# A transformer block on one core: the SSD branch's product kept in four PSUM banks over two passes of its channels

## Chip, cores, metric

One core of one Trainium2 chip. The metric is the device time of one execution in microseconds; three runs of the kernel before gave a median of 601.98 us (601.45 to 602.56).

## What is computed

One block on 256 tokens with 1024 channels, all in float32. Cut to what matters here:

```python
y_ssd  = gated_group_rmsnorm(y_ssd, z, ssd_norm)          # 2048 channels, 4 groups of 512
merged = sigmoid(gate_a) * (y_attn @ w_attn_branch) + sigmoid(gate_b) * (y_ssd @ w_ssd_branch)
x = x + merged @ w_out
x = x + hier_moe(rmsnorm(x, ffn_norm), ...)               # router, top-2 of 32 SwiGLU experts, 96 MiB of weights
```

The product `y_ssd @ w_ssd_branch` sums over 2048 channels and gives 1024 columns. The group norm of the fourth group of channels is the last thing known of its left operand.

## The kernel before

**Products in three passes.** A weight arrives raw (SP issues its transfer, L163), in pieces of 128 rows of the contracted dimension; ACT casts each piece to its high part (L174), and the remainder, the low part, is a subtraction (L178), by DVE for even pieces and by POOL for odd ones. The piece with its two parts is the tile `w_hl`. A product takes three matmuls per piece: high by high, high by low, low by high. `wide_chunk` (L302) makes 512 columns for both tiles of 128 tokens, in two PSUM banks: 8 pieces x 2 token tiles x 3 passes = 48 matmuls. It runs them in an order in which the second token tile follows the first by some pieces.

**The SSD branch's product S** (L842 to L865). Four wide chunks, in the order (i=0, c=0), (i=0, c=1), (i=1, c=0), (i=1, c=1): i is the half of the 2048 channels, c the half of the 1024 columns. Here they are called S1 to S4. `tab[t, c]` holds, for token tile t, the attention branch's part `ta` and the gate's tanh `tb`. For every chunk and token tile DVE computes `mg = (tb + 1) * ps` from PSUM (L848). For i=0 POOL adds that to `ta` in SBUF (L850). For i=1 DVE adds `ta` (L852), PE transposes the sum in four steps into a PSUM bank `ps_mT` (L855), and ACT and DVE split that into `mT` (L860, L861), the left operand of the next product.

**The last group's norm** (`ssd_tail`, L781 to L800) runs while S1 and S2 do, since only S3 and S4 need it: PE sums squares (`ps_n`, L785), DVE scales (`nv`, L787), POOL takes the power -1/2 (L101), PE spreads the result over the partitions (`ps_r`, L791), DVE multiplies (`yg`, L797) and splits (`yT`, L800).

**The product with w_out** (L886 to L928), names `ps_o`: 512 columns as a wide chunk (c=0), then 256 (c=2) and 256 (c=3, one token tile after the other). DVE adds each to x (`x_sb`, L889, L909), ACT squares the sum for the norm (`sqo`, L913), PE transposes it (`ps_hf`, L917), ACT and DVE scale it (`xT`, L923, L921), PE forms the router's logits (`ps_lg`, L927).

**Routing and experts** (from L951). Per token tile a chain of small DVE operations: the sum of squares (`ms`, L954), an inverse root by three Newton steps (names `fr0`, `fr1`, L112 to L123), `logit` (L956), maxima, `sel`, ranks on PE (`ps_rk`), slots (`Dm`, L976). Then for eight groups of four experts PE gathers tokens (L1046), multiplies by the gate and up weights (`pgu`, L1053) and the down weights (`py`, L1113). The experts' weights (`we`, L292) come through SP's queue into buffers that earlier tiles give back: the transfer into a buffer waits until its last reader is done.

**PSUM** has 8 banks: three behind the tag "mm" (pool `pmm`, in rotation) and five by name (pool `pacc`: acc00, acc01, acc10, acc11, pgu). `ps_mT` uses acc10 for t=0 and pgu for t=1, `ps_lg` acc00, `ps_hf` acc01 (and acc11 for c=3, t=1).

**Order of the work.** The program names tiles and operations; a scheduler sets the order on each engine from its own estimate of times, and within one engine the instructions run in that order. An edit at one place can therefore change the order on all engines after it.

Of the kernel before, what the change touches and what calls it, by code (L numbers as in the profile page):

```python
# [11 lines left out]
F32 = mybir.dt.float32  # L12
# [8 lines left out]
P = 128  # L21
T = 256
D = 1024
KD = 8
# [25 lines left out]
def block_kernel(ctx, tc, xin, idn, ngain, catt, cprep, cssd, cmoe, cwr, wsm, wwide, win, wgu, wdn, out, dbg=None):  # L50
    nc = tc.nc
    pe, act, dve, pool = nc.tensor, nc.scalar, nc.vector, nc.gpsimd
# [3 lines left out]
    pmm = ctx.enter_context(tc.tile_pool(name="pmm", bufs=3, space=PSUM))  # L56
# [87 lines left out]
    for t, k in TORD:  # L144
        i = pe.transpose(ps_h[k // 2][:, k % 2, t * P:(t + 1) * P], x_sb[:, t, k * P:(k + 1) * P], ident)
# [66 lines left out]
    for step in PRO:  # L212
        if step[0] == "g":
            g_part(int(step[1]))
        else:
            w, k = (w0 if step[0] == "0" else w1), int(step[1])
# [85 lines left out]
        mm3(tm_regions(w, src, [ps[:, t, :] for t in range(2)]))  # L302
        return ps

    def wide_chunk(name, src, lag, mid=None):


        w = pairs(next_w(), slice(0, 512))
        ps = [pmm.tile([P, 512], F32, tag="mm", name="ps_" + name) for t in range(2)]
        lhs = [pairs(src, slice(t * P, (t + 1) * P)) for t in range(2)]  # L310
        steps = sorted([(k + lag * t + 0.5 * t, t, k) for t in range(2) for k in range(KD)])
        for n, (_, t, k) in enumerate(steps):
            if n == KD and mid:
                mid()
            for i, (a, b) in enumerate(PASSES):
                pe.matmul(ps[t], lhsT=lhs[t][k][:, a], rhs=w[k][:, b], start=k == 0 and i == 0,  # L316
                          stop=k == KD - 1 and i == 2)
        return ps

    def cm_chunk(name, src=hT_all):  # L320
# [518 lines left out]
    xp = ctx.enter_context(tc.tile_pool(name="xp", bufs=NX, reuse_waits="tile"))  # L839
    pacc = ctx.enter_context(tc.tile_pool(name="pacc", bufs=1, space=PSUM, reuse_waits="tile"))  # L840

    for i in range(2):  # L842
        for c in range(2):
            ps = wide_chunk("S", yT[2 * i:2 * i + 2], LAG)
            for t in range(2):
                ta, tb = tab[t, c][:, 0], tab[t, c][:, 1]
                m = mo2.tile([P, 512], F32, tag="y", name="mg")
                dve.scalar_tensor_tensor(m, tb, 1.0, ps[t], op0=ALU.add, op1=ALU.mult)  # L848
                if i == 0:
                    pool.tensor_add(ta, m, ta)  # L850
                    continue
                dve.tensor_add(m, m, ta)  # L852
                pt = pacc.tile([P, 2, 2, P], F32, tag=("acc10", "pgu")[t], name="ps_mT")
                for k in range(4):
                    pe.transpose(pt[:, k // 2, k % 2, :], m[:, k * P:(k + 1) * P], ident)  # L855
                if t == 0:
                    mT += [bigt([P, 2, 2, T], F32R, f"mT{2 * c + j}", "G") for j in range(2)]
                for j in range(2):
                    hl = mT[2 * c + j][:, :, :, t * P:(t + 1) * P]
                    act.copy(hl[:, 0], pt[:, j])  # L860
                    dve.tensor_sub(hl[:, 1], pt[:, j], hl[:, 0].bitcast(F32))  # L861
            if i:
                prefetch(PF1[2 * c] + PF1[2 * c + 1])
# [9 lines left out]
    pool.memset(on16, 1.0)  # L873
    ssq = mo.tile([P, 2, 4], F32, name="ssq")
    pre = mo.tile([P, 2], F32, name="pre")
    ps_lg = pacc.tile([P, 2, 36], F32, tag="acc00", name="ps_lg")

    def warm2(n, after):

# [5 lines left out]
    for c in range(4):  # L885
# [4 lines left out]
        elif c == 2:  # L890
            ps = tm_chunk(next_w(), mT, "o")
# [9 lines left out]
        for ts in ((0,), (1,)) if c == 3 else ((0, 1),):  # L901
            tt = slice(ts[0], ts[-1] + 1)
            nt = len(ts)
            if c == 3:
                mm3(regions[ts[0]:ts[0] + 1])
            phf = pacc.tile([P, 2, nt, P], F32, tag=f"acc{ts[0]}1", name="ps_hf")
            xT = mo2.tile([P, 2, nt, P], F32, tag="y", name="xT")
            if c > 1:
                dve.scalar_tensor_tensor(x1[:, tt, o], ps[ts[0]].unsqueeze(1) if c == 3 else ps, 0.5, x_sb[:, tt, o],  # L909
                                         op0=ALU.mult, op1=ALU.add)  # L910
            for t in ts:
                sq = mo2.tile([P, 256], F32, tag="dc", bufs=1, name="sqo")
                act.activation(sq, x1[:, t, o], AF.Square, accum_out=ssq[:, t, c:c + 1])  # L913
            for kk in range(2):
                for t in ts:
                    k = 2 * c + kk
                    pe.transpose(phf[:, kk, t - ts[0], :], x1[:, t, k * P:(k + 1) * P], ident)  # L917
            for kk in range(2):
                k = 2 * c + kk
                if kk:  # L920
                    dve.tensor_scalar(xT[:, kk], phf[:, kk], fgain[:, k:k + 1], None, op0=ALU.mult)  # L921
                else:
                    act.activation(xT[:, kk], phf[:, kk], AF.Copy, scale=fgain[:, k:k + 1])  # L923
            for kk in range(2):
                for t in ts:
                    k = 2 * c + kk
                    last_lg = pe.matmul(ps_lg[:, t, :], lhsT=xT[:, kk, t - ts[0], :], rhs=wr[:, k, :],  # L927
                                        start=k == 0 and t == 0, stop=k == KD - 1 and t == 1)  # L928
# [93 lines left out]
        pe.transpose(ps_mr, mr, ident)  # L1022
        dve.tensor_reduce(mi, ps_mr, axis=AX.X, op=ALU.max)


    def pt_(shape, name):
        return pmm.tile(shape, F32, tag="mm", name=name)

    ring = list(etags)
    for q in range(8):  # L1030
# [292 lines left out]
```

## Time and profile before

| what | value |
|---|---|
| median of 3 runs | 601.98 us |
| profiled execution, its own time | 601.8 us |
| span of its trace | 600.0 us |
| mean granted clock | 0.982 |
| busy: PE, DVE, ACT, POOL | 562.6, 328.2, 273.5, 252.6 us |
| moved by DMA | 159.27 MB, mean 265 GB/s |

PE's matmuls cover 94% of the span, but the span has stages with different limits: projections, SSD and attention until about 320 us, S from 318 to 365 us, the product with w_out to 393 us, routing to 400 us, experts to the end. Each stage is read for itself, by the timeline of an engine and by the windows. A row of the trace with x4 for fp32 matmuls by the router, for `ps_n` and for `ps_r` stands for two instructions of the program.

### The profile page before, as it was taken

The page shows a single profiled execution, that of the slowest core. Times are in us where ns is not written, and L with a number is a line of the kernel's source. Part 1 is how long each engine was busy: PE and PEld are TensorE (multiplying, and loading weights), DVE is VectorE, ACT ScalarE, POOL GpSimd, SP SyncE. Part 2 cuts the span into 40 slices and gives each one's busy share as a digit, 9 for nine tenths or more (in the row PEclk, how much of TensorE's full clock was granted, in tenths as well). Part 3 has the DMA queues.
Part 4 walks back from the last instruction along what each step waited for, and adds up shares of the span by engine and source line. Part 5 has one row for each costly group of instructions (what it writes and reads, how often), then busy time and mean ns, then how long its engine had stood idle before and what let it go on. Part 6 is the DMA issues. An engine that isn't in the chain of part 4 may idle for free.

```text
span 600.0 us, 9955 instructions
## 1 busy us (share of the span) xinstructions
PE 562.6 (94%) x3605; PEld 403.0 (67%) x3605; DVE 328.2 (55%) x705; ACT 273.5 (46%) x633; POOL 252.6 (42%) x256
## 2 busy tenths in 40 slices
PE   8999999999999998999999999999988898896986
PEld 5878768799898996899877777963543452340412
DVE  4459975799994768789786676462112111210101
ACT  7467557658885768768774445410000000000001
POOL 4897695675854345565677764300000000000000
PEclk9999999999999997999999999999989999997999
DMA  6745245363344467343737669999999999999994
GB/s 264 245 156 170 94 143 176 108 205 127 125 137 145 135 217 330 106 157 130 276 126 298 213 225 415 389 336 416 421 414 412 419 417 414 413 419 419 411 415 175
DMA packets 35811, 159.27 MB, mean 265 GB/s; under 512 B 4144, under 2 KB 5808, under 8 KB 27184
## 3 DMA queue, kind: packets, MB, share of 16 engines
q1 hardware_dynamic: 34464, 157.30, 69.6%
q10 hardware_dynamic: 1296, 1.30, 0.7%
q8 instruction: 30, 0.49, 0.3%
q14 instruction: 21, 0.17, 0.1%
HBM read 157.54 MB, written 1.05 MB: 264 GB/s over the span
## 4 chain that ended last, share of the span: by engine, by line
PE 51%; DMA 28%; DVE 7%; POOL 6%; issue 4%; ACT 3%; ACTq 0%; SPq 0%; POOLq 0%; DVEq 0%
DMA we<-wgu 19%; PE ps_xs L263 8%; PE ps_z L263 8%; PE ps_g L316 5%; DMA we<-wdn 4%; PE ps_A L316 4%; POOL w_hl L178 3%; DMA w_raw<-wwide 3%; PE pgu L1053 2%; PE ps_q L316 2%; PE ps_S L316 2%; PE ps_o L263 2%; PE py L1113 2%; DVE w_hl L178 2%; PE po L565 2%
## 5 line engine op out<-in xcount | busy, mean ns | idle before, releaser
L178 POOL TENSOR_TENSOR w_hl<-w_raw,w_hl 128x512 fp32r<-128x512 f32 (+1 forms) x107 | 153.6, 1441 | 75.4 <-ACT w_hl L174 57.0
L174 ACT CAST w_hl<-w_raw 128x512 fp32r<-128x512 f32 (+1 forms) x212 | 125.8, 618 | 63.3 <-DMA w_raw<-wwide 16.3
L178 DVE TENSOR_TENSOR w_hl<-w_raw,w_hl 128x512 fp32r<-128x512 f32 (+1 forms) x105 | 97.5, 931 | 44.4 <-ACT w_hl L174 43.8
L1053 PE MATMUL pgu<-we,xg 128*32 128x512 f32 x512 | 65.6, 616 | 4.9 <-DMA we<-wgu 4.8
L1071 POOL TENSOR_TENSOR dc<-Dm,cmr 128x128 f32<-128x128 f32 x16 | 6.1, 401 | 147.8 <-DVE Dm L976 132.2
L263 PE MATMUL ps_xs<-hT,w_hl 128*128 128x256 f32 x384 | 52.6, 290 | 0.0
L316 PE MATMUL ps_g<-w_hl,gT 128*128 128x512 f32 x192 | 49.5, 400 | 1.6 <-POOL w_hl L178 1.4
L263 PE MATMUL ps_z<-hT,w_hl 128*128 128x256 f32 x384 | 50.8, 285 | 0.0
L263 PEld LDWEIGHTS ps_xs<-hT,w_hl 128*128 128x128 f32 x384 | 49.0, 196 | 2.6 <-issue 2.6
L263 PEld LDWEIGHTS ps_z<-hT,w_hl 128*128 128x128 f32 x384 | 47.5, 191 | 0.7 <-issue 0.7
L316 PE MATMUL ps_S<-w_hl,yT 128*128 128x512 f32 x192 | 45.5, 393 | 1.4 <-DVE w_hl L178 1.4
L1053 PEld LDWEIGHTS pgu<-we,xg 128*32 128x32 f32 x512 | 15.3, 111 | 43.6 <-issue 26.1
L316 PEld LDWEIGHTS ps_g<-w_hl,gT 128*128 128x128 f32 x192 | 34.9, 188 | 11.2 <-POOL w_hl L178 1.9
L316 PEld LDWEIGHTS ps_S<-w_hl,yT 128*128 128x128 f32 x192 | 35.7, 188 | 9.6 <-DVE w_hl L178 1.9
L1049 DVE TENSOR_TENSOR xg<-ps_g,cmoe 128x512 f32<-128x512 f32 (+2 forms) x18 | 11.4, 631 | 56.1 <-PE ps_g L1046 56.0
L1046 PEld LDWEIGHTS ps_g<-Dm,x_sb 128*128 128x128 f32 x256 | 31.0, 191 | 15.0 <-issue 11.3
L1091 DVE SCALAR_TENSOR_TENSOR ac<-th,pgu 128x256 f32<-128x256 f32 x8 | 3.4, 421 | 63.3 <-ACT th L1089 63.3
L1113 PE MATMUL py<-we,aTt 128*32 128x512 f32 (+1 forms) x272 | 34.0, 626 | 3.8 <-DVE aTt L1099 2.1
L1046 PE MATMUL ps_g<-Dm,x_sb 128*128 128x128 f32 x256 | 33.4, 280 | 0.0
L1124 ACT COPY y<-py 128x512 f32<-128x512 f32 (+1 forms) x9 | 4.9, 539 | 61.7 <-PE py L1113 61.7
L1089 ACT ACTIVATE th<-pgu,rs 128x256 f32<-128x256 f32 x8 | 3.8, 474 | 63.1 <-PE pgu L1053 63.1
L1128 PE MATMUL acc<-y,dcT 128*128 128x512 f32 (+1 forms) x68 | 30.7, 577 | 1.7 <-DVE y L1126 1.6
(308 smaller groups left out, 978.8 us busy)
## 6 DMA issues: line engine op xcount, KB each, us to landing
we<-wgu SPq DMA_DIRECT2D x42, 1024.0 KB, 13.9
w_raw<-wwide SPq DMA_DIRECT2D x60, 512.0 KB, 3.9
we<-wdn SPq DMA_DIRECT2D x25, 1024.0 KB, 13.8
w_raw<-win SPq DMA_DIRECT2D x44, 512.0 KB, 3.6
we<-wgu SPq DMA_DIRECT2D x44, 512.0 KB, 10.6
we<-wdn SPq DMA_DIRECT2D x14, 512.0 KB, 10.2
x_sb<-xin SPq DMA_DIRECT2D x2, 512.0 KB, 4.4
w_raw<-wsm SPq DMA_DIRECT2D x1, 512.0 KB, 5.7
```

Source lines behind the costliest of these rows:

```text
L174: return act.copy(self.hl[i][:, 0], self.raw[i])
L178: return eng.tensor_sub(hl[:, 1], self.raw[i], hl[:, 0].bitcast(F32))
L263: pe.matmul(ps, lhsT=lhs[k][:, a], rhs=rhs[k][:, b], start=j == 0 and k == 0 and i == 0, stop=j == len(regions) - 1 and k == KD - 1 and i ...
L316: pe.matmul(ps[t], lhsT=lhs[t][k][:, a], rhs=w[k][:, b], start=k == 0 and i == 0, stop=k == KD - 1 and i == 2)
L565: pe.matmul(po[64 * jj:64 * jj + 64], lhsT=v_sb[:, kt, j * HD:(j + 1) * HD], rhs=PTs[jj][kt], start=kt == 0, stop=kt == t)
L1046: pe.matmul(ps[:, kk, :], lhsT=x1[:, t, (k + kk) * P:(k + kk + 1) * P], rhs=Dm[:, t].rearrange("p e j -> p (e j)"), start=t == 0, stop=t == 1)
L1049: dve.tensor_tensor(xg[:, ks, :], ps, fgain[:, ks].unsqueeze(2).to_broadcast([P, n, P]), op=ALU.mult)
L1053: i = pe.matmul(pgu[32 * e:32 * e + 32, :], lhsT=xg[:, k, 32 * e:32 * e + 32], rhs=wg[k][e], start=k == 0, stop=k == KD - 1, tile_position ...
L1071: pool.tensor_tensor(dc[:, t], Dm[:, t], cmr[:, t, 4 * q:4 * q + 4].unsqueeze(2).to_broadcast([P, 4, NSLOT]), op=ALU.mult)
L1113: i_py = pe.matmul(py[32 * e:32 * e + 32, :], lhsT=aTt[:, f, 32 * e:32 * e + 32], rhs=wd[2 * n + f][e][:, c], start=f == 0, stop=f == 1, t ...
L1124: act.copy(y, py)
L1128: pe.matmul(acc[t][n][:, c], lhsT=dcT[:, t * P:(t + 1) * P], rhs=y, start=False, stop=q == 7 and c.stop == 512)
```

## The change

The sums over i are kept in PSUM: four accumulators, `sacc[0]` in two "mm" banks for c=0 and `sacc[1]` in acc10 and pgu for c=1. A chunk of i=0 starts the sum and doesn't close it, that of i=1 goes on and closes it. The operations of L848 and L850 for i=0 go; for i=1 they stay as they were (`mg`, then the addition of `ta` by DVE). `ps_mT` moves to acc11 (t=0) and acc10 (t=1, the bank of c=1, t=0). `ps_lg` and the first `ps_hf` are only allocated earlier. Lines behind L302 shift by 4 or more.

```diff
@@ wide_chunk @@
+    def wide_chunk(name, src, lag, mid=None, into=None, part=None):
         w = pairs(next_w(), slice(0, 512))
-        ps = [pmm.tile([P, 512], F32, tag="mm", name="ps_" + name) for t in range(2)]
+        ps = into or [pmm.tile([P, 512], F32, tag="mm", name="ps_" + name) for t in range(2)]
...
-                pe.matmul(ps[t], lhsT=lhs[t][k][:, a], rhs=w[k][:, b], start=k == 0 and i == 0,
-                          stop=k == KD - 1 and i == 2)
+                pe.matmul(ps[t], lhsT=lhs[t][k][:, a], rhs=w[k][:, b], start=k == 0 and i == 0 and part != 1,
+                          stop=k == KD - 1 and i == 2 and part != 0)
@@ S @@
+    sacc = [[pt_([P, 512], f"ps_S0{t}") for t in range(2)]]
+    ps_lg = pacc.tile([P, 2, 36], F32, tag="acc00", name="ps_lg")
+    ps_hf0 = pacc.tile([P, 2, 2, P], F32, tag="acc01", name="ps_hf")
+    sacc.append([pacc.tile([P, 512], F32, tag=n, name=f"ps_S1{t}") for t, n in enumerate(("acc10", "pgu"))])
     for i in range(2):
         for c in range(2):
-            ps = wide_chunk("S", yT[2 * i:2 * i + 2], LAG)
+            ps = wide_chunk("S", yT[2 * i:2 * i + 2], LAG, into=sacc[c], part=i)
+            if i == 0:
+                continue
             for t in range(2):
                 ta, tb = tab[t, c][:, 0], tab[t, c][:, 1]
                 m = mo2.tile([P, 512], F32, tag="y", name="mg")
                 dve.scalar_tensor_tensor(m, tb, 1.0, ps[t], op0=ALU.add, op1=ALU.mult)
-                if i == 0:
-                    pool.tensor_add(ta, m, ta)
-                    continue
                 dve.tensor_add(m, m, ta)
-                pt = pacc.tile([P, 2, 2, P], F32, tag=("acc10", "pgu")[t], name="ps_mT")
+                pt = pacc.tile([P, 2, 2, P], F32, tag=("acc11", "acc10")[t], name="ps_mT")
...
-            phf = pacc.tile([P, 2, nt, P], F32, tag=f"acc{ts[0]}1", name="ps_hf")
+            phf = ps_hf0 if c == 0 else pacc.tile([P, 2, nt, P], F32, tag=f"acc{ts[0]}1", name="ps_hf")
```

The scheduler moves instructions as well, from the end of S1 on. Up to there all engines' orders are the same. Three places are shown.

**PE at the end of S1**: S1 and S2 with the norm's two small products. Before (the names yT_2054 and yT_2055 are the first half of the channels, yT_2056 and yT_2057 the second):

```order
L316 MATMUL ps_S<-w_hl,yT_2055 128x512 x14
L316 MATMUL ps_S<-w_hl,yT_2054 128x512 x4
L316 MATMUL ps_S<-w_hl,yT_2055 128x512 x4
L785 MATMUL ps_n<-ones,ysum 128x1 x2
L316 MATMUL ps_S<-w_hl,yT_2054 128x512 x8
L316 MATMUL ps_S<-w_hl,yT_2055 128x512 x4
L316 MATMUL ps_S<-w_hl,yT_2054 128x512 x11
L791 MATMUL ps_r<-ident,nv 128x128 x2
L316 MATMUL ps_S<-w_hl,yT_2054 128x512
L316 MATMUL ps_S<-w_hl,yT_2055 128x512 x16
L316 MATMUL ps_S<-w_hl,yT_2056 128x512
```

Now (ps_S_3973 and ps_S_3974 are the accumulators of c=0, ps_S_3977 and ps_S_3978 those of c=1):

```order
L320 MATMUL ps_S_3973<-w_hl,yT_2055 128x512 x2
L320 MATMUL ps_S_3974<-w_hl,yT_2055 128x512 x2
L789 MATMUL ps_n<-ones,ysum 128x1 x2
L795 MATMUL ps_r<-ident,nv 128x128 x2
L320 MATMUL ps_S_3977<-w_hl,yT_2054 128x512 x12
L320 MATMUL ps_S_3978<-w_hl,yT_2054 128x512 x3
```

Before, 23 matmuls of S2 stood between `ps_n` and `ps_r`; now `ps_r` is right behind `ps_n`, and all of S2 is behind both.

**PE at the end of the product with w_out.** Before:

```order
L263 MATMUL ps_o_4573<-w_hl,mT_4351 128x256 x3
L927 MATMUL ps_lg<-cwr,xT 128x36 x2
L263 MATMUL ps_o_4573<-w_hl,mT_4351 128x256
L927 MATMUL ps_lg<-cwr,xT 128x36 x2
L917 MATMUL ps_hf<-ident,x_sb 128x128 x4
L263 MATMUL ps_o_4573<-w_hl,mT_4351 128x256 x2
L263 MATMUL ps_o_4573<-w_hl,mT_4352 128x256 x6
L927 MATMUL ps_lg<-cwr,xT 128x36 x4
L917 MATMUL ps_hf<-ident,x_sb 128x128 x4
L927 MATMUL ps_lg<-cwr,xT 128x36 x4
```

Now (ps_o_4557 is the last token tile's sum for c=3):

```order
L263 MATMUL ps_o_4557<-w_hl,mT_4228 128x256 x4
L263 MATMUL ps_o_4557<-w_hl,mT_4337 128x256 x6
L263 MATMUL ps_o_4557<-w_hl,mT_4338 128x256 x6
L934 MATMUL ps_lg<-cwr,xT 128x36 x4
L924 MATMUL ps_hf<-ident,x_sb 128x128 x6
L934 MATMUL ps_lg<-cwr,xT 128x36 x4
L924 MATMUL ps_hf<-ident,x_sb 128x128 x2
L934 MATMUL ps_lg<-cwr,xT 128x36 x4
```

Before, the logits of c=0 to 1 and the transposes `ps_hf` of c=2 stood ahead of the last matmuls of `ps_o`; now four `ps_lg` and four `ps_hf` more are behind them.

**DVE at the same place.** Before:

```order
L119 SCALAR_TENSOR_TENSOR fr0a<-fr0y,fr0h 128x1
L921 TENSOR_SCALAR xT<-ps_hf,cmoe 128x256
L123 SCALAR_TENSOR_TENSOR fr0y<-fr0a,fr0y 128x1
L909 SCALAR_TENSOR_TENSOR x_sb<-ps_o_4573,x_sb 128x256
L119 SCALAR_TENSOR_TENSOR fr0a<-fr0y,fr0h 128x1
L123 SCALAR_TENSOR_TENSOR fr0y<-fr0a,fr0y 128x1
L971 COPY r<-fr0y 128x1
L954 TENSOR_SCALAR ms_4731<-ssq,pre 128x1
L112 TENSOR_SCALAR fr1i<-ms_4731 128x1
L116 TENSOR_SCALAR fr1h<-ms_4731 128x1
L921 TENSOR_SCALAR xT<-ps_hf,cmoe 128x128
```

Now:

```order
L113 TENSOR_SCALAR fr0y<-fr0i 128x1
L119 SCALAR_TENSOR_TENSOR fr0a<-fr0y,fr0h 128x1
L123 SCALAR_TENSOR_TENSOR fr0y<-fr0a,fr0y 128x1
L961 TENSOR_SCALAR ms_4715<-ssq,pre 128x1
L119 SCALAR_TENSOR_TENSOR fr0a<-fr0y,fr0h 128x1
L112 TENSOR_SCALAR fr1i<-ms_4715 128x1
L116 TENSOR_SCALAR fr1h<-ms_4715 128x1
L123 SCALAR_TENSOR_TENSOR fr0y<-fr0a,fr0y 128x1
L113 TENSOR_SCALAR fr1y<-fr1i 128x1
L119 SCALAR_TENSOR_TENSOR fr0a<-fr0y,fr0h 128x1
L119 SCALAR_TENSOR_TENSOR fr1a<-fr1y,fr1h 128x1
L928 TENSOR_SCALAR xT<-ps_hf,cmoe 128x256
```

Before, `xT` of c=2 (128x256) stood ahead of the last addition to x and of `ms` of the second token tile (ms_4731). Now it stands behind both (the addition is the row ahead of these, ms_4715 the second tile's sum) and behind seven steps of the two inverse roots.

## Rows read from the trace of the kernel before

**Rows 1.** The page, part 2: granted clock in tenths, GB/s; 40 slices
```profile
PEclk9999999999999997999999999999989999997999
GB/s 264 245 156 170 94 143 176 108 205 127 125 137 145 135 217 330 106 157 130 276 126 298 213 225 415 389 336 416 421 414 412 419 417 414 413 419 419 411 415 175
```

**Rows 2.** The page, part 4: the chain of waits that ended last, by line
```profile
DMA we<-wgu 19%; PE ps_xs L263 8%; PE ps_z L263 8%; PE ps_g L316 5%; DMA we<-wdn 4%; PE ps_A L316 4%; POOL w_hl L178 3%; DMA w_raw<-wwide 3%; PE pgu L1053 2%; PE ps_q L316 2%; PE ps_S L316 2%; PE ps_o L263 2%; PE py L1113 2%; DVE w_hl L178 2%; PE po L565 2%
```

**Rows 3.** Windows: length, each engine's busy time, clock, DMA share, GB/s
```profile
400.00:404.00 4.00, 4.00 (x35) 3.01 (x33) 2.02 (x13) 0.34 (x3) 0.76 (x2) 1.00 0.73 235
```

**Rows 4.** Timeline of SP: start, length (us), operation, count
```profile
390.47 12.54 SPq L292 DMA_DIRECT2D we<-wdn  x6
```

**Rows 5.** Timeline of PE, 329 to 369 us; in brackets idle time before
```profile
330.09 0.50 PE L785 MATMUL ps_n<-ones,ysum 128*128 128x1 f32 x4
345.59 14.85 PE L316 MATMUL ps_S<-w_hl,yT 128*128 128x512 f32 x64 [1.43 <-DVE w_hl L178]
360.27 1.03 PE L855 MATMUL ps_mT<-ident,mg 128*128 128x128 f32 x8
361.06 4.60 PE L316 MATMUL ps_S<-w_hl,yT 128*128 128x512 f32 x19
365.50 2.43 PE L316 MATMUL ps_o<-w_hl,mT 128*128 128x512 f32 x10
...
368.16 3.48 PE L316 MATMUL ps_o<-w_hl,mT 128*128 128x512 f32 x14 [0.23 <-POOL w_hl L178]
```

**Rows 6.** Timeline of POOL, 327 to 332 us
```profile
327.18 3.43 POOL L178 TENSOR_TENSOR w_hl<-w_raw,w_hl 128x512 fp32r<-128x512 f32 x2
...
330.87 0.71 POOL L101 TENSOR_TENSOR nv<-nv,mhalf 128x2 f32<-128x2 f32 x1
```

**Rows 7.** DVE at 336 us (timeline); the page's group of its lo parts
```profile
336.53 0.53 DVE L871 TENSOR_TENSOR trs<-cwr,ident 128x128 bf16<-128x128 f32 x1 [4.55 <-DMA cwr<-cwr]
...
L178 DVE TENSOR_TENSOR w_hl<-w_raw,w_hl 128x512 fp32r<-128x512 f32 (+1 forms) x105 | 97.5, 931 | 44.4 <-ACT w_hl L174 43.8
```

**Rows 8.** The two lines that the change drops for two chunks, all instances
```profile
L848 DVE SCALAR_TENSOR_TENSOR mg<-tab,ps_S x8: 672/675/681, 330.7 to 368.6; 128x512 f32<-128x512 f32 x8
...
L850 POOL TENSOR_TENSOR tab<-mg,tab x4: 1293/1294/1296, 332.8 to 347.5; 128x512 f32<-128x512 f32 x4
```

**Rows 9.** Timeline of PE, 390 to 402 us
```profile
390.82 0.53 PE L927 MATMUL ps_lg<-cwr,xT 128*128 128x36 f32 x4
391.18 0.63 PE L917 MATMUL ps_hf<-ident,x_sb 128*128 128x128 f32 x4
391.57 1.20 PE L263 MATMUL ps_o<-w_hl,mT 128*128 128x256 f32 x8
392.61 0.98 PE L927 MATMUL ps_lg<-cwr,xT 128*128 128x36 f32 x8
...
401.56 1.06 PE L1053 MATMUL pgu<-we,xg 128*32 128x512 f32 x8
```

**Rows 10.** Timeline of DVE, 391 to 396 us
```profile
391.17 0.15 DVE L112 TENSOR_SCALAR fr0i<-ms 128x1 int32<-128x1 int32 x1
...
391.99 0.22 DVE L119 SCALAR_TENSOR_TENSOR fr0a<-fr0y,fr0h 128x1 f32<-128x1 f32 x1
...
392.83 0.41 DVE L909 SCALAR_TENSOR_TENSOR x_sb<-ps_o,x_sb 128x256 f32<-128x256 f32 x1
...
393.89 0.21 DVE L954 TENSOR_SCALAR ms<-ssq,pre 128x1 f32<-128x1 f32 x1
...
394.60 0.34 DVE L921 TENSOR_SCALAR xT<-ps_hf,cmoe 128x128 f32<-128x128 f32 x1
...
395.58 0.25 DVE L956 SCALAR_TENSOR_TENSOR logit<-ps_lg,fr0y,cmoe 128x36 f32<-128x36 f32 x1
```

**Rows 11.** A gap on PE (timeline) and the granted clock after it (windows)
```profile
229.55 0.65 PE L765 MATMUL py<-e,xdt 128*64 128x256 f32 x4 [1.78 <-DVE e L750]
...
232.00:236.00 4.00, 4.00 (x22) 3.51 (x19) 4.00 (x11) 4.00 (x10) 0.73 (x1) 0.50 1.00 413
```

More of the change, by code (lines that the diff above doesn't have):

```diff
@@ L303, in tm_chunk, with pt_ @@
         return ps
-    def wide_chunk(name, src, lag, mid=None):
+    def pt_(shape, name):
+        return pmm.tile(shape, F32, tag="mm", name=name)
+    def wide_chunk(name, src, lag, mid=None, into=None, part=None):
         w = pairs(next_w(), slice(0, 512))
-        ps = [pmm.tile([P, 512], F32, tag="mm", name="ps_" + name) for t in range(2)]
+        ps = into or [pmm.tile([P, 512], F32, tag="mm", name="ps_" + name) for t in range(2)]
         lhs = [pairs(src, slice(t * P, (t + 1) * P)) for t in range(2)]
@@ L875, in block_kernel @@
     pre = mo.tile([P, 2], F32, name="pre")
-    ps_lg = pacc.tile([P, 2, 36], F32, tag="acc00", name="ps_lg")
     def warm2(n, after):
@@ L1023, in combine @@
         dve.tensor_reduce(mi, ps_mr, axis=AX.X, op=ALU.max)
-    def pt_(shape, name):
-        return pmm.tile(shape, F32, tag="mm", name=name)
     ring = list(etags)
```

## The prediction

> **What bounds the kernel now.** I read the 40 slices first [rows 1]. From the 28th slice on, all but the last move 411 to 421 GB/s: the experts' weights fill the DMA engines. The chain of waits says the same: its largest piece is the transfer `we<-wgu`, 19% of the span [rows 2]. So the last third is bound by bytes, and PE's busy share there is no bound.
>
> A stage bound by bytes would hide anything done ahead of it, if it never ran dry. It does. Between 400 and 404 us the DMA share is 0.73, at 235 GB/s [rows 3]. SP's queue shows why: the issues of `we<-wdn` that begin at 390.47 us take 12.54 us for six, because the last waits for a buffer until 402.7 us, when the first `pgu` matmuls, begun at 401.56 us, give back weights [rows 4, 9]. What had been issued before has landed by then. From there to the end, the remaining bytes follow the release by the first `pgu`. **So the time moves one for one with the start of `pgu`**, that is, with the chain S, product with w_out, routing, gather. Earlier prefetches gain nothing: they only make the queue run dry sooner. A gain larger than the dry spell would stop paying; none as large is in sight.
>
> In that chain PE is the engine to follow. From S1 to the last `ps_o` it runs almost without a gap: one of 1.43 us before 345.59 us, for a low part from DVE, and one of 0.23 us before 368.16 us, for one from POOL [rows 5]. DVE was late at the first because it had stood 4.55 us at `trs`, whose constants land at 336.5 us, with the parts of the weights behind it [rows 7].
>
> **The change, part by part.**
>
> *Removed work.* Four `mg` of 0.675 us on DVE, 2.7 us, and four additions of 1.293 us on POOL, 5.2 us [rows 8]. PE waited for none of the additions; the results of i=0 were wanted only at i=1, and the matmuls are the same 192. I cost this at nothing by itself: the matmuls cover it. It frees DVE and POOL for the low parts of S2 to S4, which matters only where PE waits for them: 1.43 and 0.23 us, 1.66 us at most.
>
> *PE at the end of S1.* In the row of before, four matmuls of S2 stand ahead of `ps_n` at 330.09 us. At (360.27 - 345.59)/64 = 0.229 us each [rows 5], S1 ends at 330.09 - 0.92 = 329.17 us. Now `ps_n` starts there and ends 0.50 us later, at 329.67 us. Then `nv` has to pass POOL, which is busy with low parts until 327.18 + 3.43 = 330.61 us and does the same there as before; its power takes 0.71 us [rows 6]. So it ends between 331.3 (started at once) and 331.6 us (started at 330.87 as before). The order puts `ps_r` directly behind `ps_n`, so PE has nothing to run until then: **a gap of 1.65 to 1.95 us**, where before 23 matmuls covered it. I take 1.9, since a small memset stands ahead of the power. With `ps_r` in 0.4 us, S2 starts at 332.0 us.
>
> From there 144 matmuls at 0.229 us are 33.0 us; four transposes, at (361.06 - 360.27)/8 = 0.1 us, add 0.4. S ends at 365.4 us against 365.50 us [rows 5], but four transposes more follow in the next stage (0.4 us): +0.3 us. This holds only without the stall of 1.43 us. The low part that it waited for is now behind `nv`, `yg`, half of `yT` and `trs`, with six low parts next to it; after 337.1 us, where `trs` ends [rows 7], two or three operations at the group's mean of 0.93 us [rows 7] bring the first low part by 340 us. PE wants it with its 38th matmul of S2, at 332.0 + 38 x 0.229 = 340.7 us. So no stall, by 0.7 us; with two inputs delayed it could be 1 us of stall: a bound for the range.
>
> *The banks held.* The transposes of c=0, t=1 now go to the bank of S4's first token tile, and so wait for the `mg` that empties it. The trace's price for that is one `mg`, 0.675 us [rows 8]; nine matmuls of the other token tile and seven of `ps_o` stand in between, 16 x 0.229 = 3.7 us. I put it at nothing. The Trainium skill, page "PSUM — Partial Sum Buffer", section "Summary: rules for kernel authors", says to empty PSUM promptly because it is small, which speaks against holding four banks over two chunks. By that rule the sum would be larger by up to 0.7 us; by the rows the wait lies under other matmuls, and I keep nothing.
>
> *Queues.* SP's issues stay in their order but for two experts' transfers that change places, and come up to 1.8 us earlier (the 1.43 us stall and the freed POOL); by the first part this is worth nothing.
>
> *The product with w_out.* Its 0.23 us for POOL [rows 5] should go with POOL's additions: -0.2 us (bounds -0.23 and 0).
>
> *The tail.* Before, the last `ps_o` ended at 392.61 us, where `ps_lg` follows, and `logit` started at 395.58: 2.97 us [rows 9, 10]. Now four `ps_lg` (twice 391.18 - 390.82 = 0.36 us) and four `ps_hf` (391.57 - 391.18 = 0.39 us) [rows 9] come behind the last `ps_o`, which is 1.1 us earlier. But behind it DVE goes on in this order: the addition to x; `ms` of that tile, 393.89 - 392.83 = 1.06 us later; seven steps of the roots at (391.99 - 391.17)/5 = 0.16 us, 1.1 us [rows 10]; then `xT` of c=2, some 0.5 us. That is 2.8 us after the last `ps_o`, with 0.1 us to start. Then eight more steps, 1.2 us, and two `xT` of c=3, 0.7 us: 4.7 us. From the last `xT` to `logit` the rows have 395.58 - 394.60 = 0.98 us, of which the `xT` itself is 0.34: 5.3 us. So +2.3 us, -1.1 us: +1.2 us. The two tiles' routing steps now run in pairs, and of the 6.0 us from `logit` to `pgu` [rows 9, 10] I take off 0.3 (estimate: one small step of some 0.16 us less waited for at each of two ranks). Bounds of the tail: 0, if DVE runs ahead at the roots, to +1.8 us.
>
> *Sum:* +0.3 - 0.2 + 1.2 - 0.3 = **+1.0 us**. On the profiled execution's 601.8 us that is 602.8; this execution lies 0.2 us below the median of the runs, so against the median 603.0 us. Bounds of the terms together: about -0.7 to +3 us.
>
> **The rivals.**
>
> *A. The clock falls in the new gap (slower).* PE stood still for 1.78 us before 229.55 us, amid smaller gaps, and then the granted clock was 0.50, the lower of the two levels (1.2 instead of 2.4 GHz) [rows 11]. The new gap of 1.9 us is as long. Against it: the gap of 1.43 us in S left the clock at full speed, and here PE is busy on both sides. The slice from 225 us has a clock of 0.7, a later one from 435 us 0.8 [rows 1]; with the low level at a half, that makes 6 to 9 and 3 to 6 us at it, of which half is lost. So +1.5 to +4.5 us on the forecast, 604.5 to 607.5 us, most likely about 605: PE is dense here, which speaks for the short end. [...]
>
> *B. The stalls go and nothing comes (faster).* If POOL does the power sooner, or the gap is shorter, and the tail's DVE steps hide beside PE, what remains is the 1.43 + 0.23 us saved: 601.98 - 1.66 = 600.3 us. Against it is the order on PE and DVE, which no speed of POOL mends.
>
> *C. Nothing moves.* The dry spell of the DMA is covered by other transfers, or gap and stall cancel to a tenth and the tail too: 602.0 us. Against it are rows 3 and 4: the queue really waits for `pgu`.
>
> **How the numbers follow.** Of two results of this kernel about 0.2%, 1.2 us, can be told apart: 600.8 to 603.2 us is no change. My forecast has 0.45, of which its bounds put 0.20 above 603.2 and 0.25 within. A has 0.33, all slower; B 0.13, faster; C 0.09, the same. So faster 0.13, same 0.34, slower 0.53. The time is that of the likeliest case, 603.0 us. The range 601.0 to 605.4 us holds the forecast, C and most of A; left out are most of B and the longer half of A's low clock.
>
> **What would show it.** In the changed profile: no addition on POOL in S and four `mg` instead of eight; PE idle 1.6 to 2 us in front of `ps_r`, released by POOL's power; no stall for a low part from DVE in S3; S over at 365.4 us; behind the last `ps_o` some 5 us until `logit`, with PE waiting for `xT`; `pgu` starting near 402.6 us, and the DMA's dip in 400 to 408 us deeper by as much. A granted clock under 1 between 332 and 340 us says A. The forecast is wrong if the time of `pgu` and the end do not move together, if PE has work in front of `ps_r`, or if a low part is late in S2.

## The result

The changed kernel is slower: a median of 605.92 us (602.77 to 607.73, seven runs) against 601.64 us (600.35 to 602.61, seven runs), a ratio of 1.0071 [1.0055, 1.0087], or +4.3 us. I had forecast 603.0 us with a range of 601.0 to 605.4 us: the sign was right, the size a quarter of the true one, and the time lies above the range.

The profiled execution of the changed kernel took 605.92 us, its span is 604.0 us. Its page has, in part 2, the granted clock and the GB/s of the 40 slices, and in part 4 the chain of waits, by line:

```profile
PEclk9999999999999998999999999979999997997899
...
GB/s 267 243 167 165 84 150 168 119 191 141 109 138 142 152 240 296 129 140 181 232 191 264 193 324 416 314 256 400 420 414 412 419 418 413 414 418 422 410 413 161
...
PE ps_z L263 8%; PE ps_xs L263 8%; PE pgu L1057 8%; DMA we<-wgu 7%; PE py L1117 5%; PE ps_g L320 4%; PE acc L1132 4%; PE ps_g L1050 4%; PE ps_A L320 4%; POOL w_hl L178 4%; DMA w_raw<-wwide 3%; PE ps_q L320 2%; PE ps_o L263 2%; DVE w_hl L178 2%; PE ps_w L890 2%
```

Against [rows 1] the 27th slice (393 to 408 us) moves 256 instead of 336 GB/s, and its clock is 0.7. Against [rows 2] a line is new at the chain's end: `ps_w` on PE, 2% of the span. These are the **warming matmuls** of `warm2` (L890; L883 before): behind the last `ps_lg` the program places eleven matmuls on constants whose result nobody reads, and three behind each rank. I had left them out of the prediction.

PE from the end of S1 to the start of the product with w_out, on the timeline (start, length, operation, count; in brackets the idle time before it and who ended it), which answers to [rows 5]:

```profile
327.76 0.50 PE L789 MATMUL ps_n<-ones,ysum 128*128 128x1 f32 x4
330.03 0.71 PE L795 MATMUL ps_r<-ident,nv 128*128 128x128 f32 x4 [1.77 <-POOL nv L101]
330.50 28.63 PE L320 MATMUL ps_S<-w_hl,yT 128*128 128x512 f32 x125
358.96 0.60 PE L863 MATMUL ps_mT<-ident,mg 128*128 128x128 f32 x4
...
363.75 1.75 PE L320 MATMUL ps_o<-w_hl,mT 128*128 128x512 f32 x7
365.34 0.60 PE L863 MATMUL ps_mT<-ident,mg 128*128 128x128 f32 x4
...
368.81 3.02 PE L320 MATMUL ps_o<-w_hl,mT 128*128 128x512 f32 x12 [0.80 <-DVE mT L869]
```

The gap in front of `ps_r` is there, 1.77 us, and 125 matmuls of S follow without a stop at 28.46 / 125 = 0.228 us each, as before: the stall of 1.43 us has gone. New is a wait of 0.80 us for `mT`: four transposes that ran inside S before now stand behind it, at 365.34 us.

PE in the tail, which answers to [rows 9]:

```profile
390.37 0.98 PE L934 MATMUL ps_lg<-cwr,xT 128*128 128x36 f32 x8
391.18 0.85 PE L924 MATMUL ps_hf<-ident,x_sb 128*128 128x128 f32 x6
392.38 1.25 PE L934 MATMUL ps_lg<-cwr,xT 128*128 128x36 f32 x8 [0.35 <-ACT xT L930]
393.47 0.41 PE L924 MATMUL ps_hf<-ident,x_sb 128*128 128x128 f32 x2
394.34 1.88 PE L934 MATMUL ps_lg<-cwr,xT 128*128 128x36 f32 x8 [0.46 <-ACT xT L930]
396.03 4.89 PE L890 MATMUL ps_w<-on 128*128 128x512 bf16 x11
400.71 0.23 PE L976 MATMUL ps_rk<-sel,trs 128*128 128x32 bf16 x1
...
404.33 1.07 PE L1057 MATMUL pgu<-we,xg 128*32 128x512 f32 x8
```

and on DVE, which answers to [rows 10]:

```profile
396.26 0.25 DVE L963 SCALAR_TENSOR_TENSOR logit<-ps_lg,fr0y,cmoe 128x36 f32<-128x36 f32 x1 [1.33 <-PE ps_lg L934]
...
398.39 0.19 DVE L973 TENSOR_TENSOR sel<-em,em 128x32 bf16<-128x32 f32 x1
...
400.99 0.19 DVE L977 SCALAR_TENSOR_TENSOR rk<-ps_rk,sel 128x32 f32<-128x32 f32 x1 [2.01 <-PE ps_rk L976]
```

`sel`, which the rank's matmul `ps_rk` needs, is ready at 398.39 + 0.19 = 398.58 us. `ps_rk` starts at 400.71 us: it stands behind the eleven warming matmuls on PE. DVE waits 2.01 us for it. The windows say why the eleven take so long (length; busy time of PE, PEld, DVE, ACT, POOL; then the granted clock, DMA share, GB/s):

```profile
392.00:394.00 2.00, 1.54 (x11) 1.17 (x10) 1.87 (x14) 0.41 (x2) 0.00 (x0) 1.00 1.00 404
394.00:396.00 2.00, 1.66 (x8) 1.57 (x9) 0.76 (x3) 0.55 (x2) 0.00 (x0) 0.66 1.02 414
396.00:398.00 2.00, 2.00 (x7) 0.77 (x7) 1.74 (x15) 0.00 (x0) 0.00 (x0) 0.50 1.03 410
398.00:400.00 2.00, 2.00 (x6) 0.75 (x5) 0.87 (x9) 0.00 (x0) 0.00 (x0) 0.50 1.03 410
400.00:402.00 2.00, 2.00 (x10) 0.73 (x9) 0.49 (x3) 0.00 (x0) 0.00 (x0) 0.63 0.67 266
402.00:404.00 2.00, 2.00 (x17) 1.83 (x16) 1.97 (x14) 0.49 (x3) 0.00 (x0) 1.00 0.04 16
```

From about 395 to 401 us TensorE runs at 0.50, the lower level (1.2 GHz); before, its granted clock is 1.00 from 392 to 400 us. What stands ahead of the fall is a PE that waits: 0.35 and 0.46 us for `xT`. Eleven warming matmuls take 4.89 us here. Before, they take 2.54 us and are over when `sel` comes, so that PE waits for it and not the other way round:

```profile
395.37 2.54 PE L883 MATMUL ps_w<-on 128*128 128x512 bf16 x11
398.09 0.18 PE L969 MATMUL ps_rk<-sel,trs 128*128 128x32 bf16 x1 [0.18 <-DVE sel L966]
```

Other executions of the changed kernel ran at a lower clock too, though no trace shows where: the mean granted clocks of the seven have a median of 0.973, and only the fastest (602.77 us) has 0.982, as the profiled execution of the kernel before.

Between 402 and 404 us, where before the queue ran dry for a moment [rows 3], the DMA stands still: share 0.04, 16 GB/s. SP's row shows the same wait as [rows 4], 16.29 us for 12.54 us:

```profile
389.50 16.29 SPq L292 DMA_DIRECT2D we<-wdn  x6
```

**The account.** Each line is a difference of starts on the timelines of the two profiled executions, S1's end being the start of `ps_n` in the new order and 330.09 us less four matmuls in the old one:

| stretch | before | now | difference | forecast |
|---|---|---|---|---|
| end of S1 to end of S | 36.32 | 35.99 | -0.33 | -0.1 |
| to the end of the last `ps_o` | 27.11 | 26.62 | -0.49 | -0.9 |
| to `logit` | 2.97 | 5.89 | +2.92 | +2.3 |
| to the first `pgu` | 5.98 | 8.07 | **+2.09** | **-0.3** |
| sum | 72.38 | 76.57 | +4.19 | +1.0 |

(The forecast's terms of the four transposes, the product and the four `ps_lg` and `ps_hf` that left it are sorted by stretch: 0.4 - 0.2 - 1.1 = -0.9.) The sum is close to the +4.3 us measured, in part by luck. Outside of these stretches the two executions differ too: S1 ends 1.4 us earlier now (327.76 for 329.18 us), and from the first `pgu` to the end it takes 199.7 us for 198.5, 1.2 us more. The two nearly cancel, which leaves +4.0 us between the spans. In all twelve traces of this document S1 ends between 327.8 and 329.2 us, with and without the change. Of the 3.2 us that I missed in the stretches, 2.4 us lie between `logit` and `pgu`.

### The profile page after: what moved, and what is told of

Its sections match the earlier page's. It is cut to its first block, busy times and chain, and to the rows that moved or that the text cites. A ratio compares the mean times of both kernels' runs of the same rounds, so it can differ in the third digit from the quotient of the medians.

```text
span 604.0 us, 9946 instructions
## 1 busy us (share of the span) xinstructions
PE 565.4 (94%) x3605; PEld 403.5 (67%) x3605; DVE 323.2 (54%) x701; ACT 273.2 (45%) x633; POOL 246.2 (41%) x252
## 4 chain that ended last, share of the span: by engine, by line
PE 64%; DMA 11%; DVE 8%; POOL 7%; issue 6%; ACT 3%; ACTq 0%; SPq 0%; POOLq 0%; DVEq 0%
PE ps_z L263 8%; PE ps_xs L263 8%; PE pgu L1057 8%; DMA we<-wgu 7%; PE py L1117 5%; PE ps_g L320 4%; PE acc L1132 4%; PE ps_g L1050 4%; PE ps_A L320 4%; POOL w_hl L178 4%; DMA w_raw<-wwide 3%; PE ps_q L320 2%; PE ps_o L263 2%; DVE w_hl L178 2%; PE ps_w L890 2%
## 5 line engine op out<-in xcount | busy, mean ns | idle before, releaser
L1132 PE MATMUL acc<-y,dcT 128*128 128x512 f32 (+1 forms) x68 | 32.5, 605 | 1.7 <-DVE y L1130 1.6
```

The source lines that it names most:

```text
L1132: pe.matmul(acc[t][n][:, c], lhsT=dcT[:, t * P:(t + 1) * P], rhs=y, start=False, stop=q == 7 and c.stop == 512)
```

## The experiments

**My theory:** the loss comes from the order of the tail and what the clock makes of it. **Rivals:** the gap at `ps_r` and the bank held in S (the change itself); the number of warming matmuls alone. The letters A, B and C in the expectations stand for this theory and such rivals, not for those of the prediction. A ratio is to the kernel before, timed again with each group of experiments (medians 601.43 us for 1, 2, 3 and 5, 601.88 us for 4, 6, 7 and 8, 601.48 us for 9 and 10); it can differ from the quotient of the two medians, most in experiment 4, by 0.0016.

*1. The tail in the old order.* The changed kernel, with two edges that bind the last eight `ps_o` matmuls behind the transposes of c=2, and the last addition to x behind `xT` of c=2.

```diff
-                mm3(regions[ts[0]:ts[0] + 1])
+                mm3(regions[ts[0]:ts[0] + 1], tail=hf_2 if ts[0] else None)
...
+                with tc.issue_after(xT_2) if ts[0] else ExitStack():
```

> The changed kernel, with two orders restored in its tail by edges between instructions: the last eight matmuls of ps_o behind the transposes ps_hf of c=2, and the addition to x of c=3, t=1 behind xT of c=2 on DVE. S stays as changed. Theory A (the loss is made in the tail: xT of c=2 late on DVE, PE idle, clock down, the eleven warming matmuls at half rate, the rank's matmul queued behind them): last ps_o to logit 3.0 us, logit to first pgu 6.0 us, clock 1.00 from 390 to 402 us, time 601.0 to 602.0 us, ratio to before 0.998 to 1.001. Rival B (the loss is made in S, by the gap at ps_r, the stall for mT and the held banks): 604.5 to 606 us, ratio 1.005 to 1.008. Rival C (the eleven warming matmuls alone hold up the rank, whatever the order ahead of them): 604 to 605 us.

Measured: 603.17 us, 1.0019 [1.0005, 1.0034], more than the theory's 0.998 to 1.001 and less than rival B's. The clock in the tail stayed at 1.00, `logit` came 2.97 us after the last `ps_o`, the warming took 2.54 us, `pgu` came 5.98 us after `logit`: all as in the kernel before. So, by the ratios, 3.1 of the 4.3 us go with the tail's order. What is left is in S: now the clock did fall in the gap at `ps_r`. Timeline of PE, then windows:

```profile
330.32 0.99 PE L796 MATMUL ps_r<-ident,nv 128*128 128x128 f32 x4 [1.77 <-POOL nv L101]
330.96 30.05 PE L321 MATMUL ps_S<-w_hl,yT 128*128 128x512 f32 x125
...
370.42 3.03 PE L321 MATMUL ps_o<-w_hl,mT 128*128 128x512 f32 x12 [0.53 <-DVE mT L870]
```

```profile
328.00:332.00 4.00, 2.23 (x12) 1.91 (x12) 1.15 (x4) 0.62 (x1) 3.51 (x4) 0.83 0.77 228
332.00:336.00 4.00, 4.00 (x15) 3.21 (x14) 2.50 (x6) 1.24 (x2) 0.00 (x0) 0.75 0.71 229
```

The same 125 matmuls take 30.05 instead of 28.63 us, after the same gap of 1.77 us. That is rival A of the prediction, at 1.4 us, or 1.6 us from the end of S1 to the end of S (37.59 for 35.99), in another execution than the first.

*2. The tail's gaps filled.* The changed kernel with its new tail order kept; two unread matmuls behind the transposes of c=2 and three behind those of c=3, t=0, so that PE doesn't stand still.

```diff
+            if c > 1:
+                fill(FILL.get((c, ts[0]), 0), hf_i)
...
+FILL = {(2,0):2,(3,0):3}
```

> The changed kernel, DVE's order untouched, with five more warming matmuls on PE where it waits in the tail: two behind ps_hf of c=2, three behind ps_hf of c=3, t=0. It tells the clock from the order. Theory A: the clock stays at 1.00, the eleven warming matmuls take 2.5 us again instead of 4.9, the rank's matmul comes 2.0 us sooner; what DVE's order itself costs, some 1.5 to 2 us, stays: 603 to 604 us, ratio 1.002 to 1.004. Rival B: no change, 605 to 606 us. If the clock had nothing to do with it (order alone), 605.5 to 606.5 us.

Measured: 604.33 us, 1.0039 [1.0022, 1.0056], as the theory expected, and that with the clock down at `ps_r` again (0.73 between 332 and 336 us). Five more matmuls make the kernel faster than the change by 0.0032, some 1.9 us. The windows and the rank:

```profile
392.00:396.00 4.00, 4.00 (x31) 3.16 (x30) 3.45 (x23) 1.36 (x5) 0.00 (x0) 1.00 1.01 357
396.00:400.00 4.00, 3.96 (x24) 2.25 (x23) 3.18 (x25) 0.25 (x1) 0.00 (x0) 1.00 1.03 411
```

```profile
397.12 2.54 PE L890 MATMUL ps_w<-on 128*128 128x512 bf16 x11
399.71 0.18 PE L985 MATMUL ps_rk<-sel,trs 128*128 128x32 bf16 x1
```

The clock stays at 1.00, the eleven take 2.54 us, `ps_rk` follows at once, and from `logit` to `pgu` it is 5.62 us, 0.36 less than before. The -0.3 of the prediction was right at full clock, and only there.

*3. Fewer warming matmuls.* The changed kernel with four instead of eleven.

```diff
-WARM = (9, 3, 10, 11, 3, 3)
+WARM = (9, 3, 10, 4, 3, 3)
```

> The changed kernel with 4 instead of 11 warming matmuls ahead of the rank's matmul. Theory A: the clock is down before them; the four are over by about 398 us, so the rank starts when sel is there (2.0 us sooner), but PE then idles and the clock stays low for longer, so that the gather and the first pgu run at half rate and 1 to 2 us are lost again: 604.5 to 606 us. Rival C (only the queue of eleven in front of the rank): 603.5 to 604 us, clock as before. Rival B: 605 to 606 us.

Measured: 606.14 us, 1.0074 [1.0052, 1.0096], no better than the change. The rank no longer waits for them, but the clock is still low when the gather comes:

```profile
398.00:400.00 2.00, 1.30 (x4) 0.30 (x2) 1.93 (x20) 0.00 (x0) 0.00 (x0) 0.50 1.02 401
400.00:402.00 2.00, 1.99 (x8) 0.79 (x8) 1.11 (x6) 0.00 (x0) 0.00 (x0) 0.50 1.03 412
```

So the number of warming matmuls alone isn't the fault. With fewer of them PE idles 0.71 us ahead of `ps_rk`, the clock stays down, and what follows pays: the three warming matmuls behind each rank take 1.44 us (0.81 before), the gather's first sixteen matmuls 2.32 us (1.95 before). From `logit` to `pgu` it is 7.22 us. This trace, too, has the fall at `ps_r` (0.61 between 332 and 336 us).

*4. The new tail alone.* The kernel before, S untouched, with the order of the changed kernel's tail on PE and DVE (the roots of both tiles ahead of `xT` of c=2; the logits of c=1 and all that follows behind the last `ps_o`).

```diff
...
+        elif c == 3:
+            with tc.issue_after(last_o[0].ins):
+                logits(1, (0, 1), xT_1)
+                logits(2, (0, 1), turn(2, (0, 1), first_a["fr1"].ins))
...
```

> The kernel before, its S untouched, with the tail's order of the changed kernel: the logits of c=1 and the transposes of c=2 behind the last ps_o, xT of c=2 on DVE behind the addition to x of c=3, t=1 and the first steps of both inverse roots. Theory A (the tail alone makes most of the loss): last ps_o to logit 5.3 to 5.9 us instead of 3.0, the clock falls near 395 us, the warming matmuls take up to 4.9 us and the rank waits for them: ratio to before 1.004 to 1.006, 603.8 to 605 us. If the clock stays up by chance of when the gaps come, ratio 1.002. Rival (the tail needs the changed S in front of it to lose): 601 to 602 us.

Measured: 603.09 us (602.09 to 605.5), 1.0036 [1.0019, 1.0053]: slower, by about 2.2 us (1.2 us by the medians), with no other part of the change, and somewhat less than the 1.004 to 1.006 expected. Its profiled execution is among its fastest (602.34 us) and kept the clock at 1.00, in spite of the same waits of 0.35 and 0.46 us on PE:

```profile
392.64 1.25 PE L946 MATMUL ps_lg<-cwr,xT 128*128 128x36 f32 x8 [0.35 <-ACT xT L939]
...
394.59 1.25 PE L946 MATMUL ps_lg<-cwr,xT 128*128 128x36 f32 x8 [0.46 <-ACT xT L939]
395.67 2.54 PE L887 MATMUL ps_w<-on 128*128 128x512 bf16 x11
```

In this trace the new order costs next to nothing: from S1's end to `pgu` it is 72.54 us, 0.16 us more than before, because the product with w_out is 1.75 us and the stretch behind `logit` 0.36 us shorter, against 2.28 us more between them. Why the median is slower all the same stays open. It suggests itself that the clock fell in the slower executions, of which no trace was taken, but their mean clocks don't bear it out: the median of the eleven is 0.979, against 0.980 in the kernel before; the three slowest (604.47 to 605.5 us) have 0.979, 0.978 and 0.976, and the second fastest (602.15 us) has 0.975.

*5. The gap at `ps_r` filled with S's own matmuls.* Experiment 1, and the accumulators of c=1 in a PSUM pool of their own, opened ahead of the norm's product, so that matmuls of S2 can stand between `ps_n` and `ps_r` as before.

```diff
...
+    paccs = ctx.enter_context(tc.tile_pool(name="paccs", bufs=1, space=PSUM, side="right", reuse_waits="tile"))
...
+    sacc.append([paccs.tile([P, 512], F32, tag=n, name=f"ps_S1{t}") for t, n in enumerate(("acc10", "pgu"))])
...
```

> As the run with the tail's order restored, and the two accumulators of c=1 in a PSUM pool of their own that opens before the norm's product, so that 25 matmuls of S2 stand between ps_n and ps_r. The gap of 1.77 us at ps_r should go. Theory: S from the end of S1 to the first ps_o 1.4 to 1.8 us shorter than in the changed kernel, and as the stall of 1.43 us of before stays away as well, 599.6 to 600.6 us, ratio to before 0.997 to 0.999. If the low parts on DVE are late again in S3, as before, 601 to 602 us.

Measured: 601.16 us, 0.9996 [0.9984, 1.0008], no gain on the kernel before, where 0.997 to 0.999 was expected. The gap is gone (25 matmuls in it) and S takes 34.12 us, 2.2 less than before. But the product with w_out takes 29.33 us, 2.2 more:

```profile
364.48 1.66 PE L323 MATMUL ps_o<-w_hl,mT 128*128 128x512 f32 x6 [0.50 <-POOL w_hl L180]
...
369.36 3.06 PE L323 MATMUL ps_o<-w_hl,mT 128*128 128x512 f32 x12 [1.42 <-DVE mT L874]
```

What S gained, the next stage gave back: 1.92 us of it in these two waits, the larger one for `mT`, with the bank still held.

*6. The gap filled with unread matmuls.* Experiment 1, and seven matmuls of S's size between `ps_n` and `ps_r`.

```diff
...
+            with tc.issue_after(n_i.ins):
+                for _ in range(7):
+                    pe.matmul(ps_w, lhsT=yT[0][:, 0, 0, 0:P], rhs=yT[0][:, 0, 0:2, :], start=True, stop=True)
```

> As the run with the tail's order restored (ratio 1.0019), with seven matmuls of the size of S between ps_n and ps_r, whose result is not used, so that PE is busy for the time in which it waited for POOL's power (1.77 us). The wait itself stays. If the clock's fall behind this gap cost what it looked like there (125 matmuls of S2 to S4 in 30.05 us against 28.63 in an execution whose clock stayed up, and 0.3 us at ps_r), the clock stays at 1.00 from 328 to 344 us and the ratio comes to 0.999 to 1.0005. If the gap only cost its idle time: 1.0015 to 1.0025.

Measured: 602.72 us, 1.0021 [1.0006, 1.0036]. The clock stays at 1.00 and the first `pgu` comes 71.80 us after S1, 0.6 less than before, so the trace does what was expected, and the time does not: it is the one expected if the gap costs its idle time alone. Its profiled execution loses 2.9 us behind `pgu` (201.3 us to the end, 198.5 before), where between 580 and 590 us the DMA share is 0.79 (0.93 before) and the clock 0.86 (1.00 before). Why is left open, and with it whether the clock's fall at `ps_r` costs the kernel any time.

*7. A free bank for the transposes, gap kept.* Experiment 1, with `ps_mT` of c=0, t=1 in acc01.

```diff
-                pt = pacc.tile([P, 2, 2, P], F32, tag=("acc11", "acc10")[t], name="ps_mT")
+                pt = pacc.tile([P, 2, 2, P], F32, tag="acc11" if t == 0 else ("acc01", "acc10")[c], name="ps_mT")
```

> As the run with the tail's order restored, and ps_mT of c=0, t=1 in bank acc01 instead of the held acc10; the gap at ps_r stays. Theory: the stall of 0.53 us for mT goes and nothing else changes: ratio to before 1.0005 to 1.0015, 601.7 to 602.4 us. If the bank was not the reason: 1.0019 as without the edit.

Measured: 603.26 us, 1.0024 [1.0008, 1.004]. The eight transposes are back inside S (362.01 us) and no `ps_o` waits for `mT`, but the clock fell at `ps_r` (0.58 between 332 and 336 us) and S took 38.01 us. The time can't be told from experiment 1's; the 1.0005 to 1.0015 expected were not reached.

*8. All three.* Experiments 1, 5 and 7 together.

> As the run without the gap (tail's order restored, accumulators of c=1 in a pool of their own), and ps_mT of c=0, t=1 in bank acc01, which is free then, instead of acc10, which S4's first token tile holds to its end. Theory: the transposes of c=0, t=1 come within S4 again, as in the kernel before, and the stall of 1.42 us of ps_o for mT (and most of the 0.50 us for a low part from POOL) goes: 599.3 to 600.3 us, ratio to before 0.9965 to 0.9985. If the held bank was not the reason: as without this edit, 0.9990 to 1.0002.

Measured: 601.74 us, 1.0008 [0.9992, 1.0024], not the gain expected. The wait for `mT` is gone, and the next one is there. First PE's timeline, then DVE's:

```profile
371.27 0.66 PE L867 MATMUL ps_mT<-ident,mg 128*128 128x128 f32 x4 [1.24 <-DVE mg L864]
```

```profile
366.06 1.78 DVE L864 TENSOR_TENSOR mg<-mg,tab 128x512 f32<-128x512 f32 x1
367.76 0.68 DVE L863 SCALAR_TENSOR_TENSOR mg<-tab,ps_S 128x512 f32<-128x512 f32 x1
368.36 1.17 DVE L180 TENSOR_TENSOR w_hl<-w_raw,w_hl 128x512 fp32r<-128x512 f32 x1
369.45 1.76 DVE L864 TENSOR_TENSOR mg<-mg,tab 128x512 f32<-128x512 f32 x1
```

From 364 to 373 us DVE has no idle time; it is the bound at that turn, and it is slow there: its additions take 1.78 and 1.76 us while POOL runs four low parts in a row beside them (from 364.29 us, 6.37 us). In experiment 5 the second of these additions took 0.68 us at 369.23 us, when POOL had nothing to do.

*9. The old stall, without the change.* The kernel before; only `trs`, which needs late constants and stood on DVE ahead of S's low parts [rows 7], is moved behind the last `mT` of S.

```diff
...
-    dve.tensor_sub(trs, C("tri2"), ident)
+    with tc.issue_after(mT_i.ins):
+        dve.tensor_sub(trs, C("tri2"), ident)
```

> The kernel before with one instruction moved: trs on DVE, which waits for constants until 336.5 us with low parts queued behind it, comes after the last mT of S. All other orders are those of before, the experts' too. The stall of 1.43 us in S3 should go. If the end follows the first pgu one for one on the early side as well: 600.4 to 600.8 us, ratio to before 0.9972 to 0.9982. If before already stands where the bytes and PE's chain of the experts meet, so that an earlier pgu gains little: 0.9990 to 1.0005.

Measured: **599.2 us (598.2 to 600.18), 0.9962 [0.9948, 0.9975]**, faster than both kernels, and by more than the 0.9972 to 0.9982 expected. S runs without the stall:

```profile
335.68 22.50 PE L316 MATMUL ps_S<-w_hl,yT 128*128 128x512 f32 x98
...
363.25 5.61 PE L316 MATMUL ps_o<-w_hl,mT 128*128 128x512 f32 x24
```

From S1's end to `pgu` it is 70.07 us, 2.31 less, and the time falls by 2.3 us: one for one on the early side too. By differences of starts S is 1.76 us shorter and the product 0.54 us; the rows of the kernel before list these two waits as 1.43 and 0.23 us of idle time, which is less than their removal gave.

*10. The end against `pgu`.* The kernel before, with the third pass of five of the eight pieces left out in `ps_o` for c=2 and c=3: 20 matmuls of the narrow shape fewer; the output lacks these terms.

```diff
+                    if i == 2 and k < skip:
+                        continue
...
+SKIP = 5
```

> The kernel before, in which the third pass (low by high) of five of the eight pieces is left out in the products ps_o of c=2 and c=3: 20 matmuls of 0.119 us less, so that its output lacks these terms. The first pgu comes 2.0 to 2.4 us sooner, with S untouched. One for one: 599.6 to 600.0 us, ratio 0.996 to 0.9968. If the early side is bounded by PE's chain of the experts: 0.9985 to 1.0005, with more bytes moved by 420 us than before and the DMA's last stretch idle for it.

Measured: 600.94 us, 0.9989 [0.9971, 1.0007]. The product is 2.9 us shorter, but its tail was put in another order too, PE waited 0.33 and 0.46 us for `xT`, the clock fell (0.76 between 394 and 398 us), and the eleven took 4.08 us:

```profile
392.81 4.08 PE L885 MATMUL ps_w<-on 128*128 128x512 bf16 x11
396.73 0.18 PE L971 MATMUL ps_rk<-sel,trs 128*128 128x32 bf16 x1
```

So `pgu` came only 1.0 us earlier after S1, and the time fell by 0.7 us, which is within the noise. It therefore doesn't test what an earlier `pgu` is worth; experiment 9 does. The same loss as in the change shows up in a kernel that has nothing else of it.

## Where the prediction was right, and where it failed

- **What bounds the kernel** held. The end follows `pgu`: over eleven of the twelve traces (all but experiment 6) the stretch from the first `pgu` to the end is 198.5 to 199.7 us, while `pgu` itself moves over 6.1 us (398.76 to 404.86 us). It held to about 1 us only: that stretch is shortest in the kernel before and longest in the change.
- **Removed work**, at nothing, is not contradicted: with the gap, the tail and the bank each put right (experiment 8) the change gives 1.0008 [0.9992, 1.0024]. A new wait of 1.24 us is left in that trace, so that the work's worth by itself is not shown.
- **PE at the end of S1** held: a gap of 1.77 us for 1.65 to 1.95, no stall in S, 0.2 us better than summed. But it doesn't take the change to remove the stall: moving one instruction (experiment 9) does it without the gap.
- **The banks held**, at nothing, was wrong by 0.80 us in the change and up to 1.42 us elsewhere. I counted the matmuls that lie between; what I didn't count is that the transposes then come behind S, where DVE has an addition of 1.78 us and a low part of 1.77 us ahead of `mT` (from 364.36 to 367.83 us in the change's trace). With a free bank (experiments 7 and 8) no `ps_o` waited for `mT`. But the held bank alone doesn't make the wait: in experiments 3 and 6, with the same transposes behind S, the addition took 0.69 us and no `ps_o` waited (see the last section). The rule that I set aside, to empty PSUM promptly (the Trainium skill, page "PSUM — Partial Sum Buffer", section "Summary: rules for kernel authors"), pointed the right way.
- **The tail**, +2.3 us from the last `ps_o` to `logit`, came out at +2.92; at full clock (experiment 4) it is 5.25 - 2.97 = +2.28 us. The rest is the last `ps_lg` at half rate, 1.88 for 1.25 us.
- **The failed step is the routing term**, "of the 6.0 us from `logit` to `pgu` I take off 0.3": it measured +2.09. At full clock it is -0.36 (experiments 2 and 4). I had PE wait for `xT` in that tail and priced all that follows at full speed; I did not look at what stands on PE between `logit` and the rank. There stand eleven warming matmuls, whose 2.54 us fit before `sel`, and whose 4.89 us don't. From the last `ps_o` to `pgu` it is 8.95 us before, 10.9 us in the new order at full clock (experiments 2 and 4) and 13.96 us in the change: 3.1 us of it is what the low clock cost there.
- **Rival A** had the right mechanism in one of two places. The clock fell in the tail, where I had priced PE's waits at full speed. At `ps_r`, where I placed it, it stayed up in the change's profiled execution and fell in experiments 1, 2, 3 and 7. There it stretched the matmuls by some 1.4 us (30.05 for 28.63), just under the low end of the price that I gave. That the kernel's time pays for it is not shown (experiment 6).
- **Rival B** and **C** are out: 1.0071 [1.0055, 1.0087].

How much of the 4.3 us each place has is known only roughly: the tail alone 2.2 us [1.1, 3.2] (experiment 4, whose trace doesn't show where), all but the tail 1.1 us [0.3, 2.0] (experiment 1). Why the scheduler chose the new tail is open; that S became shorter in its own estimate is a guess, and wasn't tried.

## What to carry to other kernels

An edit's own terms can be summed well and the time still be missed, when the scheduler re-sorts a stage far behind it: read the new order up to the next point that the time hangs on, and of every engine there, with the fillers in its queue. Where PE gets new waits, price what follows at half rate as well, above all what stands in one queue ahead of a small matmul that others wait for. And a stall that an edit happens to remove should be looked for by itself: here one instruction with a late operand, moved behind the work that doesn't need it, gave 2.3 us, and the rewrite of the accumulation gave nothing.

## What was unexpected of the hardware

- The same wait on PE lets the clock fall in one execution and not in another. A gap of 1.77 to 1.78 us in front of `ps_r` left it at 1.00 in the change's trace and took it down in four other traces (0.58 to 0.75 between 332 and 336 us). Waits of 0.35 and 0.46 us in the tail took it to 0.50 in the change and in experiment 3, waits of 0.33 and 0.46 us did so in experiment 10 (0.51 between 394 and 396 us), and the first pair left it at 1.00 in experiment 4. The Trainium skill warns of idle gaps between bursts of matmuls (page "TensorE: Matmul & The Clock Gate", section "HAM oscillation — how this bites in real kernels"), and its example there has waits for DMA of some 3 to 5 us. The traces agree that gaps can cost the clock, here even gaps shorter than in that example, and show that one trace without a fall doesn't prove a gap harmless.
- DVE and POOL slow each other. In the change's trace the addition of 128x512 on DVE (L860) took 1.78 us, with POOL's low parts beside it (two from 363.90 us, 3.37 us, so 1.69 us each), and the next one 0.68 us at 368.68 us, with POOL idle; a low part of POOL's with DVE idle for nearly all of it took 1.28 us (371.22 us).

```profile
364.36 1.78 DVE L860 TENSOR_TENSOR mg<-mg,tab 128x512 f32<-128x512 f32 x1
...
368.68 0.68 DVE L860 TENSOR_TENSOR mg<-mg,tab 128x512 f32<-128x512 f32 x1
```

It went with who began first. In the change the first addition began 0.46 us behind POOL's pair, in experiments 1 and 2 0.46 and 0.33 us behind it, and it took 1.78 us each time; in experiments 3 and 6 it began 0.11 and 0.23 us ahead of the pair (at 365.89 and 363.57 us) and took 0.69 us.
